# Eight more tokens take their rows of v by gather, and the dense product with v is 168 tokens wide instead of 176

## The chip, the core and the metric

The kernel runs on one core of a Trainium2 chip. The core has a matrix engine (TensorE, PE in the profile, with its weight loads as PEld), a vector engine (VectorE, DVE), an activation engine (ScalarE, ACT), a general engine (GpSimd, POOL) and a queue engine (SyncE, SP). Sixteen DMA engines move data between HBM, the chip's main memory, and SBUF, the core's working memory. TensorE adds up its products in PSUM. The metric is the device time of one execution in microseconds; the number to compare with is the median of several executions.

## The reference, cut to what matters

One decoder layer for 256 tokens of width 1024. A mixer (retention and block attention, merged) comes first. Then each token retrieves experts: 8 heads, 16 experts for each head, out of 16384 experts, each one row of a table u and one row of a table v.

```python
q = (ht @ w_q).reshape(T, PEER_HEADS, 2, half)
s = einsum('thcd,hcnd->thcn', q, sub_keys)
...                                  # top 16 of each half, then top 16 of the sums
experts = take_along_axis(cand_i, pos); gates = softmax(top_s)
u = u_tab[ec]                        # rows of u for the token's 128 experts
a = gelu(einsum('td,thkd->thk', hc, u))
return einsum('thk,thkd->td', gc * a, v_tab[ec])
```

The layer's output is the residual stream plus this last sum.

## The kernel before

**Two ways for one sum.** A token's experts can be fetched row by row (a gather: an indirect DMA that puts 128 rows of 4 KB into the 128 partitions), or the token can go through the dense part, where the whole table passes through the core and TensorE multiplies it with all dense tokens; experts that the token didn't choose get weight zero. The kernel does both. Of its 256 tokens, `NG` = 64 are gathered in u and in v. `NX` = 64 more are gathered in u only, in `NXG` = 4 groups of `NXP` = 16 tokens; one of those groups (`NXV` = 1), the last 16 tokens of the first tile of 128, is gathered in v too. So `NA` = 128 tokens go through the dense product with u, and `ND` = 256 - 64 - 16 = 176 through the dense product with v.

**Gathers.** For the 64 fully gathered tokens one transfer covers one of `NJ` = 64 list positions: 64 tokens and two heads fill the 128 partitions. For a group of 16 tokens the partitions are 8 heads x 16 tokens, and 16 transfers cover the 16 experts of each head. So `NU` = 64 + 64 = 128 transfers fetch rows of u, and `NV` = 64 + 16 = 80 fetch rows of v. Each moves 128 rows of 4 KB, 512 KB. `eg` holds the row numbers, `av` the weights, one column for a transfer. `fetch` (L1049) issues a transfer on GpSimd's queue into one of `RING` = 6 buffers. `gather_step` (L1108) is one step of the sequence: a fetch, and the use of the oldest buffer. For u that is a dot product on VectorE (L1064), for v a weighted sum into an accumulator (L1152): `acc` for the 64 tokens, `accx` for the group of 16, whose first term is written by ScalarE (L1149). Steps are put into the program at a pace, `GATHER` per chunk of the u stage and `GATHER_V` = 0.65 per chunk of the v stage. `later` runs small actions a given number of steps after they were asked for (`after`).

**Small rearrangements.** The lists and gates of the 64 group tokens go through DRAM to change from tokens in partitions to heads x tokens in partitions: `eix` to `eg` (L991, L1089), `gx` to `gg` (L1027, L1097), and the finished weights back into `gates` (L1078, L1083), since three of the four groups use them in the dense product with v. All on GpSimd's queue.

**Dense u stage** (loop L1308). For each of 128 chunks of 128 experts: SP loads 512 KB of u into one of `RAWS` = 6 tiles of `raw_ring`, TensorE transposes it (L730, unless it was turned early) and multiplies it with 128 tokens (L1324), two chunks to a PSUM bank. `HELD` chunks of u are loaded earlier into unused space of W, from chunk row `HELD0`. Meanwhile `dense_gates` (L1208) builds the matrix of gates, 4 tokens a step, 46 rounds of the loop for 176 tokens: one-hot rows on VectorE (L1191, L1194) and ScalarE (L1198), eight small bf16 matmuls (L1249, L1250), and gelu(u h) times gate goes to W, a tile of 128 chunks x `ND` tokens. From chunk row `SCRATCH` on, W serves as scratch space for the choice of the top 16.

**Dense v stage** (loop L1360). For each chunk c: SP loads 512 KB of v (L677) into a raw tile or, from chunk 14 on, into one of two spare places in W that are used up by then, in turns of eight. `cut_v` (L1286) splits the chunk into a high and a low part (ScalarE L151, VectorE L152), two chunks ahead; `cut_w` (L1292) does so with two chunks of W (L1296, L1297). TensorE then does 8 blocks of 128 output columns: one matmul of 2 x `ND` columns (L1356), one of `ND` columns with the low part (L1357), which add up in 8 PSUM banks all through the stage. For the 6 pairs of chunks in `PLAIN` nothing is split: one fp32 matmul of `ND` columns for each block (L1354), straight from the raw tile, which stays taken until then. SP's queue is in order: a load waits for its tile and holds up the next.

**End.** At `FOLD` = 104 the two halves of `acc` are added and written. At chunk 123 any sums left are done and rows of the residual stream are loaded. At chunk 125 eight matmuls with `pick` (L1396) sum `accx` over the 8 heads of each token into PSUM columns beside the others. Then the last two chunks are done block by block, with the turning back, the residual sum and the output.

Of the kernel before, what the change touches and what calls it, by code (L numbers as in the profile page):

```python
# [11 lines left out]
F32 = mybir.dt.float32  # L12
# [10 lines left out]
P = 128  # L23
S = 256
# [9 lines left out]
NXV = 1  # L34
NX = NXP * NXG
NA = S - NG - NX
ND = S - NG - NXP * NXV
RING = 6
GATHER_V = 0.65
GATHER = 1.04  # L40
GATHER_G = 1.14
RAWS = 6
# [3 lines left out]
BUDGET = 1.5  # L46
GSTEP = 2.05
LAG_G = 2
SCRATCH = 88
TOPK = 16  # L50
HELD = [0, 1, 2, 8, 14, 21] + list(range(26, 62, 6)) + [61, 66]
HELD0 = 2
FOLD = 104
TURNED = list(range(10, 38, 2)) + [39, 41, 43, 46, 48, 51, 53, 56, 58, 60, 63, 65, 67, 70]
NPRE = len(TURNED)
# [24 lines left out]
def layer_kernel(ctx, tc, x, mix_norm_g, w_in, ret_w_branch, moba_q_gain, moba_k_gain, moba_w_branch,  # L80
# [788 lines left out]
    av = tk.tile([P, NJ + NX], F32, name="av")  # L869
    eg = tk.tile([P, NJ + NX], I32, name="eg")  # L870
# [196 lines left out]
    def weights_x():  # L1067

        c = slice(NJ, NU)
        gs["x"] = 0  # L1070

        def nonlinear():
            A.activation(av[:, c], av[:, c], AF.Gelu)
            after(2, product)

        def product():
            V.tensor_tensor(av[:, c], av[:, c], gg[:, c], op=OP.mult)
            nc.gpsimd.dma_start(gx[1].rearrange("n h i k -> (h i) n k"), av[:, c].rearrange("p (n k) -> p n k", n=NXG))  # L1078
            after(2, back)

        def back():
            for n in range(NXV, NXG):
                nc.gpsimd.dma_start(x_rows(gates, n), gx[1][n].rearrange("h i k -> i h k"))  # L1083
            gs["xdone"] = True

        after(1, nonlinear)

    def experts_x():
        nc.gpsimd.dma_start(eg[:, NJ:].rearrange("p (n k) -> p n k", n=NXG), eix.rearrange("n h i k -> (h i) n k"))  # L1089

# [17 lines left out]
    def gather_step():  # L1108
# [35 lines left out]
        if weighed and gs["sum"] < gs["v"] and (gs["v"] - gs["sum"] == RING or gs["v"] == NV):  # L1144
            j = v_order[gs["sum"]]
            r = gs["rows"].pop(j)
            if j == NJ:
                gs["accx"] = a = tk.tile([P, D], F32, name="accx", tag="hx")
                A.activation(a, r, AF.Copy, scale=av[:, j:j + 1])  # L1149
            else:  # L1150
                a = gs["acc" if j < NJ else "accx"]
                V.scalar_tensor_tensor(a, r, av[:, j:j + 1], a, op0=OP.mult, op1=OP.add)  # L1152
            gs["sum"] += 1

    V.memset(pick[:, :32 - NXP], 0.0)
    V.tensor_reduce(pick[:, 32 - NXP:], ident.rearrange("p (h i) -> p i h", i=NXP), axis=AX.X, op=OP.add)
    V.tensor_copy(iota4, iota[:, :, None].to_broadcast([P, NK, 4]))
    held = list(HELD)

# [200 lines left out]
    for c in range(NK):  # L1360
# [26 lines left out]
        if c == NK - 5:  # L1387
            while gs["sum"] < NV:
                gather_step()
            r0b, r1 = spare(3), spare(4)  # L1390
            nc.gpsimd.dma_start(r0b[:half], x1d[NG:P - NXP, 0, :])
            nc.gpsimd.dma_start(r1, x1d[:, 1, :])
        if c == NK - 3:
            for b in range(KC):
                s = slice(b % 4 * 32, b % 4 * 32 + 32)
                T.matmul(o[b // 4][s, 2 * ND:2 * ND + P], pick, gs["accx"][:, b * P:(b + 1) * P], start=False, stop=True,  # L1396
                         skip_group_check=True)

    back = {}

# [5 lines left out]
    def turn_back(b):  # L1406
        t = back.pop(b)
        n = slice(b * P, (b + 1) * P)
        T.transpose(o[b][:, :P], t[:, :P], ident)
        T.transpose(o[b][:half, P:2 * P], t[:, P:P + half], ident)  # L1410
        V.tensor_tensor(r1[:, n], r1[:, n], o[b][:, :P], op=OP.add)
        V.tensor_tensor(r0b[:half, n], r0b[:half, n], o[b][:half, P:2 * P], op=OP.add)
        if b < 2:
            V.tensor_tensor(rx[:, b], rx[:, b], o[b][:, 2 * ND:2 * ND + P], op=OP.add)
        if b == 1:
            dst = out_flat[P - NXP:P, :].rearrange("i (q j d) -> j i q d", q=2, j=4)
            for j in range(4):
                nc.gpsimd.dma_start(dst[j], rx[32 * j + 32 - NXP:32 * j + 32])
        if b in (3, 5, 7):
            d = slice({3: 0, 5: 512, 7: 768}[b], P * (b + 1))  # L1420
            nc.sync.dma_start(out_flat[P:, d], r1[:, d])
            q = nc.scalar if b == 7 else nc.sync
            q.dma_start(out_flat[NG:P - NXP, d], r0b[:half, d])

    for b in range(KC):
        for c in (NK - 2, NK - 1):
# [59 lines left out]
```

## Time and profile before

| what | value |
|---|---|
| median of 3 executions | 931.07 us (930.93 to 934.0) |
| the profiled execution, its own time | 932.75 us |
| its span, first to last instruction | 931.0 us |
| mean granted clock of TensorE | 0.998 |
| busy: TensorE / VectorE / ScalarE / GpSimd | 921.5 / 802.5 / 510.9 / 451.0 us |
| moved by DMA | 333.03 MB, 358 GB/s over the span |
| first fetch of v / last fetch of v | 618.1 us / 890.7 us |
| dense u stage, first and last L1324 | about 302 to 641 us |
| dense v stage up to the pick matmuls | about 641 to 919 us |

The profile is of one execution, so a sum of its parts is compared with 931.0 and 932.75, and then with the median. Busy time counts an engine's instructions; a busy TensorE can still be one that waits inside a stream for its next weights. DMA share is the mean busy share of 16 DMA engines. A row of the timeline has the start, the length, the engine, the line and `out<-in`; a row of the waits has the waiting engine and line, what ended the wait, the sum, the count and the longest. "To landing" is the time from the issue of a transfer to the arrival of its last data.

### The profile page before, as it was taken

Reading aid. Unit: us, or ns where it says so; the run is one execution under the profiler, and the core shown is the slowest. Engines: PE = TensorE matmul, PEld = TensorE weight load, DVE = VectorE, ACT = ScalarE, POOL = GpSimd, SP = SyncE. Lnnn points to the kernel's source line nnn. Section 1 sums busy time; section 2 is a strip of 40 time slices with the busy share of each in tenths; the row PEclk is TensorE's granted clock in tenths of the full one; section 3 lists DMA queues with packets and bytes.
Section 4 is the critical chain, followed back from the end, with each engine's and each line's share of the span. In section 5 each row is a group of like instructions: output and inputs, shape, how many; then the busy total and the mean of one; then the engine's idle time right before and its main releaser. Section 6 shows DMA issues by size and latency. Waiting matters only on the chain.

```text
span 931.0 us, 18728 instructions
## 1 busy us (share of the span) xinstructions
PE 921.5 (99%) x6952; PEld 874.4 (94%) x6952; DVE 802.5 (86%) x1539; ACT 510.9 (55%) x938; POOL 451.0 (48%) x420
## 2 busy tenths in 40 slices
PE   9999999999999999999999999999999999999998
PEld 6878888888999999999999999999999999999997
DVE  6658866988879999999899999975999989898996
ACT  5535665534653435434677777775454545454543
POOL 3527324232102447434576687873656554455540
PEclk9999999999999999999999999999999999999999
DMA  9999989999899999999999999999999999999991
GB/s 316 203 295 313 338 299 291 329 345 333 291 366 405 401 379 354 375 380 348 407 401 405 404 384 405 403 388 340 381 399 408 409 404 410 384 409 368 387 391 61
DMA packets 108265, 333.03 MB, mean 358 GB/s; under 512 B 12460, under 2 KB 16469, under 8 KB 108046
## 3 DMA queue, kind: packets, MB, share of 16 engines
q1 hardware_dynamic: 65532, 185.17, 55.3%
q0 software_dynamic: 37824, 129.57, 38.0%
q10 hardware_dynamic: 4818, 17.09, 4.8%
q8 instruction: 55, 0.90, 0.4%
q14 instruction: 36, 0.29, 0.1%
HBM read 313.88 MB, written 19.43 MB: 358 GB/s over the span
## 4 chain that ended last, share of the span: by engine, by line
PE 94%; DMA 5%; ACT 0%; POOL 0%; DVE 0%; issue 0%; SPq 0%; DVEq 0%; ACTq 0%
PE acc L1324 24%; PE side L730 10%; PE acc L1356 9%; PE side L1356 9%; PE acc L234 6%; PE acc L235 6%; PE acc L236 6%; PE acc L1357 4%; PE side L1357 4%; DMA raw_ring<-in_w_in_dram 4%; PE acc L244 2%; PE acc L243 2%; PE acc L245 2%; PE side L1354 2%; PE acc L1354 2%; PE acc L1250 1%
## 5 line engine op out<-in xcount | busy, mean ns | idle before, releaser
L1053 POOL DMA_INDIRECT rows<-in_peer_u_dram,eg x86 | 109.0, 1267 | 72.9 <-DVE rows L1064 27.0
L1053 POOL DMA_INDIRECT rows<-in_peer_v_dram,eg x54 | 97.1, 1799 | 76.6 <-DVE vacc L1152 58.7
L730 PE MATMUL side<-ident,raw_ring 128*128 128x128 f32 x688 | 92.3, 277 | 1.3 <-DMA raw_ring<-in_peer_u_dram 1.3
L730 PEld LDWEIGHTS side<-ident,raw_ring 128*128 128x128 f32 x688 | 83.4, 192 | 1.5 <-issue 1.5
L1296 ACT ACTIVATE cw<-W 128x352 fp32r<-128x352 f32 x58 | 28.9, 499 | 74.7 <-PE acc L1357 74.7
L1198 ACT ACTIVATE oh_buf<-oh_more,tS 128x128 bf16<-128x128 f16 x176 | 58.4, 416 | 0.7 <-DVE oh_more L1191 0.5
L1064 DVE SCALAR_TENSOR_TENSOR rows<-rows,h 128x1024 f32<-128x1024 f32 x44 | 55.0, 1260 | 1.4 <-DMA rows<-in_peer_u_dram,eg 1.4
L1324 PE MATMUL acc<-hTd,raw_ring 128*128 128x128 f32 x448 | 54.6, 275 | 0.0
L1152 DVE SCALAR_TENSOR_TENSOR vacc<-rows,av,vacc 128x1024 f32<-128x1024 f32 x42 | 53.7, 1279 | 0.1
L1324 PEld LDWEIGHTS acc<-hTd,raw_ring 128*128 128x128 f32 x448 | 52.3, 192 | 0.0
L1297 DVE TENSOR_TENSOR cw<-W,cw 128x352 fp32r<-128x352 f32 x58 | 30.2, 521 | 20.0 <-ACT cw L1296 19.5
L740 POOL DMA_DIRECT2D h<-in_peer_u_dram x40 | 21.9, 552 | 44.3 <-DVE hTf L744 32.5
L1282 POOL TENSOR_TENSOR W<-W,gl 128x256 f32<-128x256 f32 (+21 forms) x32 | 26.7, 833 | 29.4 <-ACT gl L1281 24.6
L740 POOL DMA_DIRECT2D eraw<-in_peer_u_dram x40 | 22.0, 555 | 27.3 <-DVE eT L744 16.5
L1191 DVE TENSOR_TENSOR oh_more<-iota,tI 128x1024 f16<-128x1024 f16 x44 | 34.3, 780 | 0.0
L1194 DVE TENSOR_TENSOR oh_buf<-oh_more,tM 128x1024 f16<-128x1024 f16 x44 | 33.0, 751 | 0.0
L1250 PE MATMUL acc<-oh_buf 128*128 128x128 bf16 x176 | 24.4, 219 | 0.0
L1249 PE MATMUL acc<-oh_buf 128*128 128x128 bf16 x176 | 24.4, 219 | 0.0
L1265 ACT ACTIVATE W<-acc 128x512 f32<-128x512 f32 (+22 forms) x44 | 17.3, 392 | 12.8 <-PE acc L1250 11.7
L1284 ACT ACTIVATE W<-acc 128x256 f32<-128x256 f32 (+21 forms) x53 | 18.5, 349 | 5.5 <-PE acc L1324 5.4
L1249 PEld LDWEIGHTS <-oh_buf 128*128 128x128 f16 x176 | 19.8, 114 | 0.0
L1250 PEld LDWEIGHTS <-oh_buf 128*128 128x128 f16 x176 | 19.7, 114 | 0.0
(2599 smaller groups left out, 3394.2 us busy)
## 6 DMA issues: line engine op xcount, KB each, us to landing
raw_ring<-in_peer_v_dram SPq DMA_DIRECT2D x100, 512.0 KB, 10.1
raw_ring<-in_peer_u_dram SPq DMA_DIRECT2D x86, 512.0 KB, 8.3
raw_ring<-in_w_in_dram SPq DMA_DIRECT2D x52, 512.0 KB, 7.9
raw_ring<-turned SPq DMA_DIRECT2D x28, 512.0 KB, 10.8
W<-in_peer_v_dram SPq DMA_DIRECT2D x28, 512.0 KB
raw_ring<-in_peer_w_q_dram SPq DMA_DIRECT2D x16, 512.0 KB, 9.3
W<-in_peer_u_dram SPq DMA_DIRECT2D x14, 512.0 KB, 10.7
eraw<-in_peer_u_dram POOLq DMA_DIRECT2D x40, 128.0 KB, 7.5
```

The costliest lines, as they stand in the source:

```text
L234: T.matmul(o[t], xh[:, s], wh, start=(k == 0), stop=False)
L235: T.matmul(o[t], xh[:, s], wl, start=False, stop=False)
L236: T.matmul(o[t], xl[:, s], wh, start=False, stop=(k == kc - 1))
L730: T.transpose(p[:, k * P:(k + 1) * P], r.rearrange("p (i k) -> p k i", k=KC)[:, 4 * q + k], ident)
L1053: G.indirect_dma_start(out=r, out_offset=None, in_=tab, in_offset=bass.IndirectOffsetOnAxis(ap=eg[:, j:j + 1], axis=0))
L1064: V.scalar_tensor_tensor(r, r, 1.0, h, op0=OP.mult, op1=OP.mult, accum_out=av[:, j:j + 1])
L1152: V.scalar_tensor_tensor(a, r, av[:, j:j + 1], a, op0=OP.mult, op1=OP.add)
L1198: A.activation(o1[:, j], hot[:, 0, :, j], AF.Copy, scale=tS[:, t, k + j:k + j + 1])
L1250: T.matmul(p[:, j * P:(j + 1) * P], lo, o1, start=False, stop=True)
L1324: T.matmul(pa[:, n:n + NA], uT[:, k * P:(k + 1) * P], hT[:, k], start=(c % 2 == 0 and k == 0), stop=(k == KC - 1), skip_group_check=True)
L1356: T.matmul(o[b][:, :2 * ND], vh[:, n], w, start=(c == 0), stop=False, skip_group_check=True)
L1357: T.matmul(o[b][:, :ND], vl[:, n], w[:, :ND], start=False, stop=(c == NK - 1), skip_group_check=True)
```

## The change

Eight more tokens, `NY` = `NXP` // 2, the second half of another group of 16, have their rows of v gathered. The partitions of their transfers are 2 halves of the list x 8 heads x 8 tokens, so that eight transfers cover the 16 experts of each head. `NV` goes from 80 to 88 and `ND` from 176 to 168. Their lists (`eiy`) and weights (`gy`) take six small transfers through DRAM (`halves`, `listed`, `last`). They get an accumulator of their own, `accy`, started by ScalarE, and a second `pick` that sums it over halves and heads, so 16 pick matmuls instead of 8. The gate matrix has 42 steps instead of 44. The pace `GATHER_V` goes from 0.65 to 0.71. The plain pairs are 7, 17, ... instead of 6, 16, ...; held rows start at chunk row 0 of W and the scratch space at 86; the spare places in W are counted in elements, since a chunk row of W is now 168 long. The output of the 24 tokens is written in four transfers as that of the 16 was, and the dense rows of the first tile are 40 instead of 48.

```diff
-ND = S - NG - NXP * NXV
+NY = NXP // 2
+ND = S - NG - NXP * NXV - NY
-GATHER_V = 0.65
+GATHER_V = 0.71
-SCRATCH = 88
+SCRATCH = 86
-HELD0 = 2
+HELD0 = 0
-NV = NJ + NXP * NXV
-PLAIN = [6 + 10 * i for i in range(6)]
+NV = NJ + NXP * NXV + NY
+PLAIN = [7 + 10 * i for i in range(6)]
...
-        return W[:, 6 * n:6 * n + 6, :].rearrange("p c t -> p (c t)")[:, :D]
+        return W.rearrange("p c t -> p (c t)")[:, D * n:D * n + D]
...
-    v_order = range(NV)
-    pick = tk.tile([P, 32], F32, name="pick")
+    v_order = [*range(NJ + NXP * NXV), *range(NU, NU + NY)]
+    pick = [tk.tile([P, 32], F32, name=f"pick{i}") for i in range(2)]
+    accy = tk.tile([P, D], F32, name="accy")
+
+    def halves(dst, src):
+
+        src = src[NXG - 1][:, NXP - NY:, :].rearrange("h i (b k) -> b h i k", b=2)
+        for b in range(2):
+            nc.gpsimd.dma_start(dst[b], src[b])
...
+            halves(gy, gx[1])
             gs["xdone"] = True
+            after(3, last)
+
+        def last():
+            nc.gpsimd.dma_start(av[:, NU:], gy.rearrange("b h i k -> (b h i) k"))
...
+        halves(eiy, eix)
...
             ready[gs["u"]:gs["u"]] = range(NJ, NU)
+            nc.gpsimd.dma_start(eg[:, NU:], eiy.rearrange("b h i k -> (b h i) k"))
...
-            if j == NJ:
-                gs["accx"] = a = tk.tile([P, D], F32, name="accx", tag="hx")
+            if j in (NJ, NU):
+                if j == NJ:
+                    gs["accx"] = tk.tile([P, D], F32, name="accx", tag="hx")
+                a = gs["accx"] if j == NJ else accy
                 A.activation(a, r, AF.Copy, scale=av[:, j:j + 1])
             else:
-                a = gs["acc" if j < NJ else "accx"]
+                a = accy if j > NU else gs["acc" if j < NJ else "accx"]
...
-                T.matmul(o[b // 4][s, 2 * ND:2 * ND + P], pick, gs["accx"][:, b * P:(b + 1) * P], start=False, stop=True,
-                         skip_group_check=True)
+                for a, n in zip((gs["accx"], accy), pick):
+                    T.matmul(o[b // 4][s, 2 * ND:2 * ND + P], n, a[:, b * P:(b + 1) * P], start=False, stop=True,
+                             skip_group_check=True)
```

More of the change, by code (lines that the diff above doesn't have):

```diff
@@ L170, in layer_kernel @@
     eix = dr.tile([NXG, H, NXP, TOPK], I32, name="eix")
+    eiy = dr.tile([2, H, NY, TOPK // 2], I32, name="eiy")
+    gy = dr.tile([2, H, NY, TOPK // 2], F32, name="gy")
     gx = [dr.tile([NXG, H, NXP, TOPK], F32, name=f"gx{i}") for i in range(2)]
@@ L868, in layer_kernel @@
     ei = tk.tile([P, NT, NP], I32, name="ei")
-    av = tk.tile([P, NJ + NX], F32, name="av")
-    eg = tk.tile([P, NJ + NX], I32, name="eg")
+    av = tk.tile([P, NU + NY], F32, name="av")
+    eg = tk.tile([P, NU + NY], I32, name="eg")
     gg = tk.tile([P, NJ + NX], F32, name="gg")
@@ L1083, in back @@
                 nc.gpsimd.dma_start(x_rows(gates, n), gx[1][n].rearrange("h i k -> i h k"))
+            halves(gy, gx[1])
             gs["xdone"] = True
+            after(3, last)
+        def last():
+            nc.gpsimd.dma_start(av[:, NU:], gy.rearrange("b h i k -> (b h i) k"))
         after(1, nonlinear)
     def experts_x():
-        nc.gpsimd.dma_start(eg[:, NJ:].rearrange("p (n k) -> p n k", n=NXG), eix.rearrange("n h i k -> (h i) n k"))
+        halves(eiy, eix)
+        nc.gpsimd.dma_start(eg[:, NJ:NU].rearrange("p (n k) -> p n k", n=NXG), eix.rearrange("n h i k -> (h i) n k"))
         def listed():
             ready[gs["u"]:gs["u"]] = range(NJ, NU)
+            nc.gpsimd.dma_start(eg[:, NU:], eiy.rearrange("b h i k -> (b h i) k"))
         after(3, listed)
@@ L1146, in gather_step @@
             r = gs["rows"].pop(j)
-            if j == NJ:
-                gs["accx"] = a = tk.tile([P, D], F32, name="accx", tag="hx")
+            if j in (NJ, NU):
+                if j == NJ:
+                    gs["accx"] = tk.tile([P, D], F32, name="accx", tag="hx")
+                a = gs["accx"] if j == NJ else accy
                 A.activation(a, r, AF.Copy, scale=av[:, j:j + 1])
             else:
-                a = gs["acc" if j < NJ else "accx"]
+                a = accy if j > NU else gs["acc" if j < NJ else "accx"]
                 V.scalar_tensor_tensor(a, r, av[:, j:j + 1], a, op0=OP.mult, op1=OP.add)
             gs["sum"] += 1
-    V.memset(pick[:, :32 - NXP], 0.0)
-    V.tensor_reduce(pick[:, 32 - NXP:], ident.rearrange("p (h i) -> p i h", i=NXP), axis=AX.X, op=OP.add)
+    for a, n, i in zip(pick, (32 - NXP, 32 - NXP - NY), (NXP, NY)):
+        V.memset(a, 0.0)
+        V.tensor_reduce(a[:, n:n + i], ident.rearrange("p (h i) -> p i h", i=i), axis=AX.X, op=OP.add)
     V.tensor_copy(iota4, iota[:, :, None].to_broadcast([P, NK, 4]))
@@ L1390, in layer_kernel @@
             r0b, r1 = spare(3), spare(4)
-            nc.gpsimd.dma_start(r0b[:half], x1d[NG:P - NXP, 0, :])
+            nc.gpsimd.dma_start(r0b[:half], x1d[NG:NG + half, 0, :])
             nc.gpsimd.dma_start(r1, x1d[:, 1, :])
@@ L1415, in turn_back @@
         if b == 1:
-            dst = out_flat[P - NXP:P, :].rearrange("i (q j d) -> j i q d", q=2, j=4)
+            dst = out_flat[P - NXP - NY:P, :].rearrange("i (q j d) -> j i q d", q=2, j=4)
             for j in range(4):
-                nc.gpsimd.dma_start(dst[j], rx[32 * j + 32 - NXP:32 * j + 32])
+                nc.gpsimd.dma_start(dst[j], rx[32 * j + 32 - NXP - NY:32 * j + 32])
         if b in (3, 5, 7):
@@ L1422, in turn_back @@
             q = nc.scalar if b == 7 else nc.sync
-            q.dma_start(out_flat[NG:P - NXP, d], r0b[:half, d])
+            q.dma_start(out_flat[NG:NG + half, d], r0b[:half, d])
     for b in range(KC):
```

## The prediction

> **What bounds the kernel now.** I read the page first: busy shares, the 40 slices, the shares of the chain of waits.
>
> ```profile
> span 931.0 us, 18728 instructions
> ...
> PE 921.5 (99%) x6952; PEld 874.4 (94%) x6952; DVE 802.5 (86%) x1539; ACT 510.9 (55%) x938; POOL 451.0 (48%) x420
> ...
> GB/s 316 203 295 313 338 299 291 329 345 333 291 366 405 401 379 354 375 380 348 407 401 405 404 384 405 403 388 340 381 399 408 409 404 410 384 409 368 387 391 61
> ...
> PE 94%; DMA 5%; ACT 0%; POOL 0%; DVE 0%; issue 0%; SPq 0%; DVEq 0%; ACTq 0%
> ```
>
> TensorE is hardly ever idle, so the chain runs along it. But from the middle of the span on, the DMA rate stops again and again near 405 to 410 GB/s. The change takes work from TensorE and gives work to DMA, so the question is what room DMA has in the stage that changes most, the product with v. Busy time by stretch, in the order PE, PEld, DVE, ACT, POOL, then clock, DMA share, GB/s; below it the DMA traffic of 640 to 910 us:
>
> ```profile
> 640.00:660.00 20.00, 20.00 (x152) 20.00 (x151) 18.18 (x19) 13.28 (x17) 10.82 (x7) 1.00 0.97 357
> 660.00:680.00 20.00, 20.00 (x147) 20.00 (x145) 18.10 (x18) 8.29 (x11) 12.15 (x7) 1.00 1.00 384
> 680.00:800.00 120.00, 120.00 (x877) 120.00 (x876) 110.96 (x110) 61.13 (x74) 65.17 (x36) 1.00 1.03 408
> 800.00:880.00 80.00, 80.00 (x583) 80.00 (x582) 72.61 (x73) 43.85 (x54) 44.24 (x28) 1.00 1.00 384
> 880.00:910.00 30.00, 30.00 (x219) 30.00 (x218) 29.19 (x29) 13.97 (x17) 10.53 (x8) 1.00 1.00 382
> ```
>
> ```profile
> DMA packets 29162, 105.99 MB, mean 393 GB/s; under 512 B 3313, under 2 KB 3313, under 8 KB 29137
> ```
>
> TensorE is busy all the time, so today it sets the pace. DMA held 408 GB/s for 120 us, which I take as its ceiling here. At 408 the 105.99 MB need 259.8 us of the 270, so about 10.2 us of DMA time is unused: 2.5 in the first 20 us, 1.2 in the next, 4.7 in 800 to 880, 1.9 in the last 30.
>
> **TensorE, the part removed.** For a chunk of 128 experts that isn't plain, each of 8 blocks is a pair: 352 columns (L1356), then 176 (L1357). First and last L1356 of 23 pairs in a row; then first and last of 27 intervals of 512 columns, and of 43 intervals of 256 columns, in earlier stages:
>
> ```profile
> 679.70 0.35 PE L1356 MATMUL side<-cw,rhi__7544 128*128 128x352 f32 x1
> ...
> 685.97 0.35 PE L1356 MATMUL side<-cw,rhi__7615 128*128 128x352 f32 x1
> ```
>
> ```profile
> 199.83 0.39 PE L236 MATMUL acc<-rhi__1780,rl 128*128 128x512 f32 x1
> ...
> 205.95 0.39 PE L236 MATMUL acc<-rhi__1848,rl 128*128 128x512 f32 x1
> ```
>
> ```profile
> 264.78 0.28 PE L243 MATMUL acc<-hh,rhi__2411 128*128 128x256 f32 x1
> ...
> 269.94 0.28 PE L244 MATMUL acc<-hl,rhi__2454 128*128 128x256 f32 x1
> ```
>
> A pair takes 6.27/23 = 272.6 ns. Matmuls of 512 columns follow each other at 226.7 ns, of 256 at 120.0, so a column costs 0.417 ns and a matmul 13.3 ns beside its columns. By that line 352 columns are 160 ns and 176 are 86.7, together 246.7. The pair has 26 ns more: as if the second took 112 ns. Passes of 128 fp32 columns (L730, in the fence on plain chunks below) also stand at 0.89/8 = 111 ns, whence my estimate that a matmul can't be shorter than about 112 ns here, since its next weights have to be loaded meanwhile. Then only the wide half shrinks: 16 columns, 6.7 ns a pair. If both halves shrink, it is 24 columns, 10.0 ns. With 116 such chunks of 8 pairs, that is 6.2 or 9.3 us; I take 6.2, because of those 26 ns.
>
> The Trainium skill ("TensorE: Matmul & The Clock Gate", LDWEIGHTS) gives a load of 128 weight columns as 128/1.2 = 107 ns, near the 112 ns; the same page (Back-to-back issue gap) has N/2.4 + 2.5 ns for a matmul alone, by which both halves would shrink and the stage would give 9.3 us. The pair's 272.6 ns against 225 by that formula speaks for the load.
>
> The 12 plain chunks (L1354) make two passes for each block. In the chain of waits in order of time (start, length, what), eight transposes of the u stage, a plain chunk's two rows, and the start of the next plain pair:
>
> ```profile
> 321.24 0.89 PE side L730 x8
> ...
> 667.72 1.22 PE side L1354 x8
> 668.95 1.19 PE acc L1354 x8
> ...
> 711.74 1.22 PE side L1354 x8
> ```
>
> 176 columns take 1.20/8 = 150 ns a pass, 128 take 111, so 0.8 ns a column and 6.4 ns a pass for 8 columns; 12 x 8 x 2 passes give 1.2 us. The period of 20 chunks, 711.74 - 667.72 = 44.0 us, falls to 44.0 - 144 x 0.0067 - 32 x 0.0064 = 42.9 us (42.4 if both halves shrink). Over the stage TensorE saves 6.2 + 1.2 = 7.4 us (at most 10.5).
>
> Building the gate matrix has two steps fewer, 16 bf16 matmuls. Eight follow each other in 563.13 - 562.68 = 0.45 us, so 0.9 us is saved near the end of the u stage, just before its one wait:
>
> ```profile
> 562.68 0.22 PE L1249 MATMUL acc<-oh_buf 128*128 128x128 bf16 x1
> ...
> 563.13 1.11 PE L730 MATMUL side<-ident,raw_ring 128*128 128x128 f32 x8
> ```
>
> ```profile
> PE side L730 <- DMA raw_ring<-in_peer_u_dram: 1.3, 1, 1.3
> ```
>
> TensorE may only wait longer there, for a transfer. Bounds 0 and 0.9 us; I take 0.5, the middle. The eight added pick matmuls stand at the end with nothing over them. The eight there now take 0.64 us:
>
> ```profile
> 918.69 0.64 PE L1396 MATMUL side<-accx,pick 128*32 128x128 f32 x16
> ```
>
> So at most +0.6 us, which I take (the lower bound is 0, if they overlap).
>
> **DMA, the part added.** Eight gathers of 128 rows of 4 KB are 4.19 MB: 10.3 us at 408 GB/s. 105.99 + 4.19 = 110.18 MB need 270.1 us, the whole of today's 270, and TensorE would like to be 7.4 us sooner. In steady state 20 chunks ask for 20 + 14.2 transfers, 17.9 MB in 42.9 us: 418 GB/s, over the ceiling. So TensorE's saving can't all be had. What remains is the delay that the buffers can take up: the loads may land later, against the end of the stage.
>
> ```profile
> 897.62 2.44 SPq L677 DMA_DIRECT2D raw_ring<-in_peer_v_dram  x2
> ...
> 914.89 1.04 ACT L151 ACTIVATE rhi__10040<-raw_ring 128x1024 fp32r<-128x1024 f32 x1
> ```
>
> ```profile
> DMA to landing us min/median/max: 6.6/9.1/12.1
> ```
>
> ```profile
> DMA to landing us min/median/max: 7.1/13.4/14.8
> ```
>
> The last load is issued at about 900.1 (897.62 + 2.44) and lands, by the median of 880 to 910 us (upper line), at 909.2; it is first read at 914.9, so 5.7 us could be given away. At 680 to 720 us (lower line) landings already took 13.4 us in the median and TensorE didn't wait, so delays of this size can be borne. ScalarE felt them:
>
> ```profile
> ACT rhi__7485 L151 <- DMA raw_ring<-in_peer_v_dram: 4.4, 1, 4.4
> ACT rhi__7940 L151 <- DMA raw_ring<-in_peer_v_dram: 4.2, 1, 4.2
> ```
>
> A later load is such a wait at ScalarE's cut (L151). Behind it stand the cut of W (L1296) and, on VectorE, the low part (L152) and the weighted sums; SP's next load into that tile and GpSimd's next gather wait for these. So the end is late only when the two cut chunks in hand run out. The unused 2.5 us of 640 to 660 stays, since no gather can start before sums free its buffers. The other 7.7 us can be filled, as gathers and loads both queue. The stage: 270.1 + 2.5 - 5.7 = 266.9, a gain of 3.1 us.
>
> The Trainium skill ("DMA: Bandwidth & Descriptors", Measured) has 425 GB/s for large loads; at that rate 418 GB/s would fit and TensorE's whole 7.4 us would show. The trace's 408 over 120 us, with shares of 1.03, speaks against it.
>
> **What costs nothing.** VectorE does eight more weighted sums less one (the first is ScalarE's), and 42 instead of 44 gate steps:
>
> ```profile
> L1152 DVE SCALAR_TENSOR_TENSOR vacc<-rows,av,vacc 128x1024 f32<-128x1024 f32 x42 | 53.7, 1279 | 0.1
> ```
>
> In 680 to 800 us VectorE has 110.96 of 120 busy; 54.5 chunks bring 0.06 x 54.5 = 3.3 more sums, 4.2 us, 115.2 in about 117 to 119: 97 to 98%. It fits, barely; without that cover it costs up to 7 x 1.28 = 9 us. Six small transfers on GpSimd's queue are like these:
>
> ```profile
> L991 POOL DMA_DIRECT2D eix<-ei x4: 548/553/609, 348.8 to 350.4; - x4
> ```
>
> Six times 0.55 us on a queue whose gathers run up to six ahead of their use; the two that read a list wait for landings that L1089 and L1083 wait for already, and behind them stand the next gather and the products of L1282. I take 0; uncovered, 3.3 us. The pace ends where it did: 88 sums at 0.71 a chunk are done at chunk 123, as 80 were at 0.65. The other edits (where spare tiles lie in W, which pairs are plain, the start of the held rows) move bytes between buffers; no instruction is added.
>
> **Sum.** Stage -3.1, gates -0.5, pick +0.6: -3.0 us, the span 931.0 becomes 928.0. The profiled execution took 932.75 us, 1.75 around its span and 1.68 over the median; the median 931.07 becomes 928.1.
>
> **Rivals.**
> *TensorE's pace holds.* The buffers (six raw tiles, two in W, six of rows) absorb the shortage until the gathers end. For it: no wait of TensorE in the stage even at 13.4 us of landing, and 408 may be what was asked for and not the ceiling; against: 418 over 408. Gain 7.4 + 0.9 - 0.6 = 7.7 us, 923.4; with both halves shrinking 10.8, 920.3.
> *Swallowed.* Of the 10.2 us unused, 5.5 stay: 270.1 + 5.5 - 5.7 = 269.9, so 931.0.
> *Slower: SP's queue starves DMA.* A plain chunk keeps its raw tile until TensorE is through with it, and SP, in order, waits:
>
> ```profile
> SPq L677 <- PE acc L1354: 51.9, 12, 7.3
> ```
>
> If these waits make the gaps of 800 to 880 us, and all six plain pairs, which now lie in raw tiles, make such gaps again, all 10.2 us stay: 270.1 + 10.2 - 5.7 = 274.6, with the rest +4.7, 935.8. It decides from about 6 us of kept gaps on. Against it: at 711 and 755 us a plain pair left no gap, the loads still out covered it.
>
> **How the numbers follow.** Forecast, a part of the gain (926.4 to 930): 0.47. TensorE's pace: 0.24, of it 0.04 for both halves. Swallowed (930 to 934): 0.18. Slower: 0.11. The bound of what can be told from no change is 0.5%, 4.7 us: 926.4 and 935.7. Faster is the second case and a little of the first, 0.27; slower the last, and not all of it, 0.10; same 0.63. The range 922.5 to 935.0 leaves out the both-halves case and most of the last.
>
> **What would show it.** After the change: starts of L1356 266 ns apart (262.6 would be both halves); the stage's DMA at 405 or more in nearly every stretch after 660; landings of L677 at 13 us and over late in the stage; ScalarE waiting for raw tiles past 720, and some idle TensorE at L1356. TensorE without idle time there and DMA over 415 GB/s would prove the second case; gaps at plain pairs with DMA under 395 the last.

## The result and the profile after

The kernel after takes 936.16 us (median of 15 runs, 930.08 to 941.88), the kernel before 930.55 us on the same chip (15 runs, 927.53 to 934.0). The ratio is 1.0061, with a 95% interval of 1.0043 to 1.0078: 5.6 us slower, where 928.1 and a gain of 3.0 were forecast. The profiled execution after took 941.88 us, the longest of its runs. One execution of a kernel below, "narrow only", took 2052 us and is not counted in its ratio (without it that kernel's median is 925.62). From here on "cut" means the split of a chunk by ScalarE and VectorE, and line numbers of the kernel after are used: L1376 and L1377 are the pair, L1374 the plain passes, L152 and L153 the cuts, L1171 the weighted sum, L1404 the addition at the fold, L1417 the pick. Rows of a changed kernel have its own numbers, a few lines off (L1380 and L1321 with eight loads less are L1376 and L1317 here); a kernel made from the one before has its numbers.

The page of the kernel after, busy shares, the GB/s of the 40 slices and the shares of the chain of waits:

```profile
span 940.0 us, 18745 instructions
...
PE 920.3 (98%) x6952; PEld 870.4 (93%) x6952; DVE 807.0 (86%) x1544; ACT 509.3 (54%) x929; POOL 476.2 (51%) x434
...
GB/s 307 212 282 285 336 299 302 328 351 334 282 363 402 390 394 342 375 398 338 408 407 406 401 362 407 404 389 349 405 408 408 407 408 409 408 408 409 386 375 62
...
PE 70%; DMA 18%; DVE 6%; issue 4%; ACT 1%; SPq 0%; DVEq 0%; POOL 0%; ACTq 0%; POOLq 0%
```

TensorE's share of the chain fell from 94% to 70%, and DMA's rose from 5% to 18%. In the stage of v nearly every slice now stands at 405 to 409 GB/s. The stretches of the prediction from 660 us on, with the last 40 us divided more finely (columns: PE, PEld, DVE, ACT, POOL, clock, DMA share, GB/s):

```profile
660.00:680.00 20.00, 20.00 (x150) 19.91 (x148) 19.18 (x20) 7.98 (x11) 14.38 (x8) 1.00 1.03 411
680.00:800.00 120.00, 118.56 (x881) 117.45 (x879) 114.03 (x114) 63.04 (x76) 75.64 (x38) 1.00 1.03 408
800.00:880.00 80.00, 78.58 (x581) 77.54 (x579) 74.41 (x75) 41.39 (x50) 50.68 (x31) 1.00 1.03 408
880.00:890.00 10.00, 6.15 (x43) 5.95 (x42) 7.25 (x8) 4.98 (x6) 4.81 (x3) 0.89 1.03 356
890.00:900.00 10.00, 10.00 (x61) 10.00 (x61) 7.36 (x7) 2.21 (x2) 9.21 (x4) 0.77 1.02 399
```

DMA moved 408 GB/s from 680 to 880 us without a break; before, the stretch from 800 on had 384. TensorE is no longer always busy: 1.4 us idle in each of the two long rows, and 3.85 us in 880 to 890, after which its granted clock falls to 0.89 and 0.77.

The start of every plain pair cuts the stage into periods of 20 chunks. The first pass of the first two and the last two in the timeline of the kernel after, and the first and the last row of the pick:

```profile
673.84 1.33 PE L1374 MATMUL side<-W,raw_ring 128*128 128x168 f32 x8
717.67 1.34 PE L1374 MATMUL side<-W,raw_ring 128*128 128x168 f32 x8
...
849.87 1.34 PE L1374 MATMUL side<-W,raw_ring 128*128 128x168 f32 x8
900.05 1.34 PE L1374 MATMUL side<-W,raw_ring 128*128 128x168 f32 x8
...
925.95 0.45 PE L1417 MATMUL side<-accx,pick 128*32 128x128 f32 x8
...
926.62 0.44 PE L1417 MATMUL side<-accy,pick 128*32 128x128 f32 x8
```

Four periods take 43.8 to 44.2 us, as long as before (44.0) and not 42.9. The fifth, with the fold in it, takes 50.2. From the first matmul of the stage (643.9) to the pick it is 282.1 us, against 277.4 before.

Set side by side, the two profiled executions differ by 941.88 - 932.75 = 9.1 us: the stage of v +4.7, from the pick to the end of the span 14.1 against 12.3, +1.8, the stage of u 338.5 against 339.0, -0.5, and the start of the stage of u +3.0 (305.4 against 302.4); 0.1 lies around the span. The start of the stage of u shows no effect of the change: in the profiles of the experiments that start lies between 298.0 and 301.4, with the eight tokens and without. (In both executions here TensorE's granted clock was down near 62 us: 0.66 from 60 to 65 us before, 0.68 and 0.63 from 60 to 70 us after.) Without these two 6.0 are left, about the 5.6 of the medians.

**How the fold stalls.** At chunk 104 GpSimd sends half of `vacc` (the accumulator of the 64 tokens) into W, and at chunk 107 VectorE adds it. VectorE in the timeline of the kernel after, then ScalarE, then TensorE (the brackets hold the idle time before and what ended it):

```profile
881.92 1.28 DVE L1171 SCALAR_TENSOR_TENSOR accx<-rows,av,accx 128x1024 f32<-128x1024 f32 x1
885.95 1.22 DVE L1404 TENSOR_TENSOR W<-W,vacc 64x1024 f32<-64x1024 f32 x1 [2.75 <-DMA W<-vacc]
887.09 1.21 DVE L153 TENSOR_TENSOR rlo__9675<-raw_ring,rhi__9674 128x1024 fp32r<-128x1024 f32 x1
888.23 0.49 DVE L1317 TENSOR_TENSOR cw<-W,cw 128x336 fp32r<-128x336 f32 x1
```

```profile
880.66 1.06 ACT L152 ACTIVATE rhi__9674<-raw_ring 128x1024 fp32r<-128x1024 f32 x1 [1.31 <-DMA raw_ring<-in_peer_v_dram]
```

```profile
884.50 0.35 PE L1376 MATMUL acc<-cw,rhi__9649 128*128 128x336 f32 x1
884.68 0.24 PE L1377 MATMUL acc<-cw,rlo__9650 128*128 128x168 f32 x1
888.77 0.65 PE L1376 MATMUL side<-cw,rhi__9674 128*128 128x336 f32 x1 [3.85 <-DVE cw L1317]
...
889.36 0.56 PE L1376 MATMUL side<-cw,rhi__9674 128*128 128x336 f32 x1
```

ScalarE had its half of the next chunk ready at 881.7. VectorE stood 2.75 us at L1404, then added, and only then made the low half (887.09) and cut W (888.23). TensorE, which finished the chunk before, had nothing to do for 3.85 us. After that its pairs stand about 0.5 us apart (888.77, 889.36, and on to 894.29) instead of 0.27, for some 6 us. The transfer itself was no slower than before. Tile `vacc`, its transfer and the addition, before and after:

```profile
L1378 POOL DMA_DIRECT2D W<-vacc x1: 580/580/580, 870.3 to 870.3; - x1
L1384 DVE TENSOR_TENSOR W<-W,vacc x1: 1218/1218/1218, 879.8 to 879.8; 64x1024 f32<-64x1024 f32 x1
...
  DMA W<-vacc: 1.4, 1
```

```profile
L1398 POOL DMA_DIRECT2D W<-vacc x1: 563/563/563, 876.6 to 876.6; - x1
L1404 DVE TENSOR_TENSOR W<-W,vacc x1: 1218/1218/1218, 886.0 to 886.0; 64x1024 f32<-64x1024 f32 x1
...
  DMA W<-vacc: 2.8, 1
```

From issue to addition it is 9.5 us before and 9.4 after, and the low half and the cut of W behind it are done 12.3 us after the issue before (at 882.6), 12.1 after (888.7). VectorE waited at the fold before, too, for 1.4 us. It cost nothing, because TensorE wanted that chunk only 13.0 us after the issue:

```profile
883.30 0.35 PE L1356 MATMUL side<-cw,rhi__9673 128*128 128x352 f32 x1
```

So the fold of before had 0.7 us to spare. After the change TensorE was through with the chunk ahead of it at 884.9, 8.3 us after the issue, 3.8 too soon. The stock of finished work had shrunk: in the chunks from 865 us to the fold, VectorE finished a low part 2.9 to 4.2 us ahead of TensorE's first use of it in the kernel before, and 0.3 to 1.5 us ahead after the change. ScalarE's part of the very next chunk had itself just waited 1.31 us for its load. What takes the stock away, DMA or something else, is for the experiments.

### The profile page after: what moved, and what is told of

Its sections match the earlier page's. It is cut to its first block, busy times and chain, and to the rows that moved or that the text cites. A ratio compares the mean times of both kernels' runs of the same rounds, so it can differ in the third digit from the quotient of the medians.

```text
span 940.0 us, 18745 instructions
## 1 busy us (share of the span) xinstructions
PE 920.3 (98%) x6952; PEld 870.4 (93%) x6952; DVE 807.0 (86%) x1544; ACT 509.3 (54%) x929; POOL 476.2 (51%) x434
## 4 chain that ended last, share of the span: by engine, by line
PE 70%; DMA 18%; DVE 6%; issue 4%; ACT 1%; SPq 0%; DVEq 0%; POOL 0%; ACTq 0%; POOLq 0%
PE acc L1344 23%; DMA raw_ring<-in_peer_v_dram 11%; PE side L733 9%; PE acc L237 6%; PE acc L238 6%; PE acc L239 6%; DMA W<-in_peer_v_dram 3%; DMA raw_ring<-in_w_in_dram 3%; PE side L1376 2%; PE acc L1376 2%; DVE vacc L1171 2%; PE acc L246 2%; PE acc L247 2%; PE acc L248 2%; PE acc L1270 1%
## 5 line engine op out<-in xcount | busy, mean ns | idle before, releaser
L1063 POOL DMA_INDIRECT rows<-in_peer_v_dram,eg x58 | 111.7, 1926 | 68.7 <-DVE vacc L1171 49.0
L1063 POOL DMA_INDIRECT rows<-in_peer_u_dram,eg x86 | 106.2, 1234 | 76.0 <-DVE rows L1074 31.3
L1218 ACT ACTIVATE oh_buf<-oh_more,tS 128x128 bf16<-128x128 f16 x168 | 55.8, 418 | 1.0 <-DVE oh_more L1211 1.0
L1171 DVE SCALAR_TENSOR_TENSOR vacc<-rows,av,vacc 128x1024 f32<-128x1024 f32 x42 | 53.6, 1277 | 0.1
L743 POOL DMA_DIRECT2D h<-in_peer_u_dram x40 | 21.8, 552 | 46.8 <-DVE hTf L747 33.6
L1317 DVE TENSOR_TENSOR cw<-W,cw 128x336 fp32r<-128x336 f32 x58 | 29.0, 499 | 11.7 <-ACT cw L1316 11.7
L1316 ACT ACTIVATE cw<-W 128x336 fp32r<-128x336 f32 x58 | 27.5, 474 | 16.4 <-PE acc L1377 14.9
L743 POOL DMA_DIRECT2D eraw<-in_peer_u_dram x40 | 22.0, 554 | 28.1 <-DVE eT L747 16.5
L1214 DVE TENSOR_TENSOR oh_buf<-oh_more,tM 128x1024 f16<-128x1024 f16 x42 | 30.0, 714 | 0.0
L1269 PE MATMUL acc<-oh_buf 128*128 128x128 bf16 x168 | 23.3, 219 | 0.0
L1270 PE MATMUL acc<-oh_buf 128*128 128x128 bf16 x168 | 23.3, 219 | 0.0
L1287 DVE TENSOR_TENSOR W<-acc,W 128x256 f32<-128x256 f32 (+21 forms) x32 | 16.1, 502 | 4.9 <-ACT W L1285 4.2
L996 POOL DMA_DIRECT2D eg<-ei x4 | 2.3, 564 | 34.5 <-ACT W L634 30.7
```

Source lines behind the costliest of these rows:

```text
L743: queue.dma_start(dst[32 * g:32 * g + 32].rearrange("a (b d) -> a b d", b=4), src[g])
L1063: G.indirect_dma_start(out=r, out_offset=None, in_=tab, in_offset=bass.IndirectOffsetOnAxis(ap=eg[:, j:j + 1], axis=0))
L1218: A.activation(o1[:, j], hot[:, 0, :, j], AF.Copy, scale=tS[:, t, k + j:k + j + 1])
```

## The experiments

The table has, from each kernel's profile, the time from the first matmul of the v stage to the first plain pair, the five periods of 20 chunks, the rest to the pick, and their sum, in us. Each profile is of one execution. "Ratio" is the time against executions of the kernel before on the same chip, with its 95% interval; it differs from the ratio of the two medians, by 0.2% at most.

| kernel | periods of the v stage | sum | median | ratio |
|---|---|---|---|---|
| before | 26.2, 44.0, 44.0, 44.0, 44.0, 44.0, 31.0 | 277.4 | 930.55 | |
| after | 29.9, 43.8, 44.2, 44.0, 44.0, 50.2, 25.9 | 282.1 | 936.16 | 1.0061 (1.0043 to 1.0078) |
| narrow only | 29.8, 42.8, 42.8, 42.8, 43.2, 44.5, 25.9 | 271.8 | 925.66 | 0.9937 (0.9913 to 0.996) |
| gathers only | 26.2, 44.0, 44.0, 44.0, 44.9, 46.2, 31.0 | 280.4 | 934.48 | 1.005 (1.0032 to 1.0067) |
| eight loads less | 30.0, 42.9, 43.0, 42.8, 42.8, 48.9, 25.9 | 276.2 | 930.42 | 1.000 (0.9983 to 1.0017) |
| half sums | 29.8, 42.8, 43.5, 43.8, 44.9, 50.7, 25.9 | 281.3 | 935.5 | 1.0057 (1.0034 to 1.0079) |
| fold later | 30.0, 43.7, 44.2, 43.4, 44.9, 43.8, 30.1 | 279.9 | 935.93 | 1.0082 (1.0047 to 1.0118) |
| before, fold later | 27.1, 44.0, 44.0, 44.0, 44.0, 44.0, 31.0 | 278.2 | 930.42 | 1.0003 (0.9984 to 1.0022) |
| eight loads less, fold later | 29.9, 43.1, 42.8, 42.8, 42.8, 42.8, 25.9 | 270.1 | 924.83 | 0.9952 (0.9933 to 0.997) |
| plain pairs at 6 | 25.7, 43.8, 44.0, 43.7, 44.7, 49.7, 30.1 | 281.6 | 937.37 | 1.0093 (1.0061 to 1.0125) |
| four tokens | 30.2, 43.4, 43.4, 43.4, 43.4, 48.9, 26.3 | 278.9 | 939.92 | 1.0103 (1.0088 to 1.0119) |
| four tokens, fold later | 30.9, 43.4, 43.4, 43.4, 43.4, 43.4, 27.7 | 275.6 | 935.58 | 1.0054 (1.0041 to 1.0067) |
| before, pace 0.71 | 26.3, 44.0, 44.0, 44.0, 44.0, 46.8, 31.0 | 280.2 | 934.29 | 1.004 (1.0026 to 1.0055) |
| before, pace 0.71, fold later | 26.2, 44.0, 44.8, 44.0, 44.0, 44.2, 31.0 | 278.2 | 930.97 | 1.0003 (0.9988 to 1.0019) |
| four tokens, lists later | 32.9, 43.4, 43.4, 43.4, 43.4, 43.4, 28.1 | 278.1 | 930.06 | 0.9996 (0.9984 to 1.0009) |

### One half of the change at a time

The kernel after without the eight tokens' gathers and sums, at the old pace; their part of the output is left out (`accy` is only set to zero):

```diff
-GATHER_V = 0.71
+GATHER_V = 0.65
...
-NV = NJ + NXP * NXV + NY
+NV = NJ + NXP * NXV
...
```

> The changed kernel without its eight added gathers and their sums (accy is only set to zero, so the retrieval of eight tokens is left out), paced at 0.65: the removed part alone. DMA theory (the v stage is held at 408 GB/s): 20 + 13 transfers in 42.9 us are 403 GB/s, just under the ceiling, so TensorE sets the pace and the time is 923 to 926 us against 930.5 of before. VectorE theory (it is 97% full in the changed kernel): 13 sums in 20 chunks leave it at 94%, so also 923 to 927. If the narrower product itself is no cheaper, 929 to 931.

The kernel before with eight more gathers (of rows that it fetches anyway) and their sums, which go nowhere:

```diff
-GATHER_V = 0.65
+GATHER_V = 0.71
...
-NV = NJ + NXP * NXV
+NV = NJ + NXP * NXV + 8
...
+            elif gs["sum"] > NV - 8:
+                V.scalar_tensor_tensor(r, r, av[:, j:j + 1], r, op0=OP.mult, op1=OP.add)
```

> The kernel before with eight more gathers of v rows and eight more scalings of them (into their own buffers; the result doesn't use them), paced at 0.71: the added part alone, the product still 176 wide. DMA theory: 110.2 MB need 270 us at 408 GB/s and the stage is 277 us to the pick matmuls, so there is room on average, 930 to 934 us. VectorE theory: 41.9 us in a period of 44.0 are 95%, so 930 to 932. If the added gathers cost their full 10.3 us, 940.

The narrow product alone gains 4.9 us, and its stage of v 5.6; its first periods are 42.8 us, what the prediction's 42.9 had worked out for TensorE. The gathers alone lose 3.9 us, a little more than either theory allowed, 3.0 of it in the fourth and fifth period, though TensorE's work is unchanged. So the gain is there. But the two halves do not add up: 277.4 - 271.8 = 5.6 gained and 280.4 - 277.4 = 3.0 lost would leave a gain of 2.6 in the stage of v, and measured is a loss of 4.7. A faster TensorE leaves DMA less time for the same bytes.

### What is short: bytes, VectorE, or SP's queue

Eight loads of v are left out, as many bytes as the eight gathers bring; those chunks are multiplied with their neighbour's rows:

```diff
+SKIPPED = [24, 40, 48, 64, 72, 80, 88, 104]
...
+            if c in SKIPPED:
+                v_raw[c] = v_raw[c - 1]
```

> The changed kernel with eight loads of v chunks left out, spread over the stage (those chunks use their neighbour's rows, so the product is another one): the bytes of before with all of the changed kernel's work on the engines. DMA theory: the waits for landings and TensorE's idle time at L1376 go, 923 to 927 us. VectorE theory: as the changed kernel, 934 to 938.

The weighted sums take only half of the columns, so that half of the output of the gathered tokens is missing:

```diff
-                V.scalar_tensor_tensor(a, r, av[:, j:j + 1], a, op0=OP.mult, op1=OP.add)
+                V.scalar_tensor_tensor(a[:, :D // 2], r[:, :D // 2], av[:, j:j + 1], a[:, :D // 2], op0=OP.mult, op1=OP.add)
```

> The changed kernel with the weighted sums of v rows on 512 of the 1024 columns (the other half of these tokens' retrieval is left out): VectorE has about 86 x 0.6 = 50 us less to do, the bytes are the same. DMA theory: as the changed kernel, 933 to 938 us. VectorE theory: 923 to 927.

The plain pairs stand where they stood before:

```diff
-PLAIN = [7 + 10 * i for i in range(6)]
+PLAIN = [6 + 10 * i for i in range(6)]
```

> The changed kernel with the plain pairs at 6, 16, ... as before. If the place of the plain pairs matters (a plain chunk holds its raw tile while SP waits), 2 us or more of difference, in either direction; if the bytes and the stall are all, 934 to 937 us as the changed kernel.

Bytes it is, in the ordinary periods: with eight loads less these fall to 42.8 to 43.0 us, while with half the sums they go up to 44.9 all the same, and the time is that of the kernel after. (A load left out also frees SP's queue and a raw tile for a while; no run takes away the bytes alone.) The place of the plain pairs changes nothing that these runs can tell. ScalarE's idle time before the cut of v, 640 to 920 us, by what ended it: the kernel before, after, and after with eight loads less:

```profile
  DMA raw_ring<-in_peer_v_dram: 18.0, 9
  DMA W<-in_peer_v_dram: 2.0, 2
```

```profile
  DMA raw_ring<-in_peer_v_dram: 60.6, 49
  DMA W<-in_peer_v_dram: 24.0, 13
```

```profile
  DMA raw_ring<-in_peer_v_dram: 21.4, 15
  DMA W<-in_peer_v_dram: 15.3, 9
```

The cut waits for a load 62 times after the change, instead of 11 times, and 24 times with the bytes given back. But that run still has a period of 48.9 us, the one with the fold, and so its 930.42 us lie above the 923 to 927 that the DMA theory expected.

### The fold

VectorE's addition comes six chunks later and the transfer of its result five, so that `vacc` has landed when VectorE gets there; tried on the kernel after, on the kernel before, and with eight loads less:

```diff
-        if c == FOLD + 3:
+        if c == FOLD + 9:
...
-        if c == FOLD + 8:
+        if c == FOLD + 13:
```

> The changed kernel with the add of the two halves of vacc (VectorE's wait for the transfer W<-vacc) six chunks later, at chunk 113, and the write of it at chunk 117; the same work and bytes. Theory of the stall: VectorE, in order, waits 2.8 us for that transfer, TensorE runs dry for 3.9 us and then has half its clock for 6.8 us, so about 6 us go, 928 to 931 us. Pure DMA theory: the bytes set the pace and the lost time only reappears as other waits, 934 to 937.

> The kernel before with the same move of the add from chunk 107 to 113. Both theories: there VectorE waited 1.4 us and TensorE not at all, so no difference, 929 to 932 us; if it is clearly faster, some of before's executions had that stall too.

> The changed kernel with eight loads of v chunks left out (those chunks use their neighbour's rows) and with the add moved to chunk 113. Theory of two causes, bytes and the stall at the add: with both gone TensorE sets the pace, 923 to 926 us. If the stall was only a sign of the bytes: as with the loads alone, 930.

TensorE's waits, 600 to 930 us, in the kernel after (whole span), with the fold later, with eight loads less, and with both:

```profile
PE side L1376 <- DVE cw L1317: 6.6, 8, 3.9
```

```profile
PE side L1376 <- DVE cw L1317: 5.6, 12, 1.0
```

```profile
PE side L1380 <- DVE cw L1321: 2.8, 1, 2.8
```

```profile
PE side L737 <- DMA raw_ring<-in_peer_u_dram: 1.6, 1, 1.6
```

With eight loads less, the fold alone is left, and moving it gains 930.42 - 924.83 = 5.6 us: 2.8 of waiting and the rest at the lower clock. With both gone no wait is left in the stage of v (the one in the last fence is of the stage of u), and it takes 270.1 us; TensorE's pace by the prediction was 277.4 - 7.4 = 270.0. With all the bytes, moving the fold gains nothing that these runs can tell (935.93 us, as the pure DMA theory had it): eight waits of 6.6 us in all, one of them 3.9, become twelve of 5.6 in all, none over 1.0, and the last segment is 30.1 us instead of 25.9. DMA is as late as it was, and the delay shows somewhere else. Before the change the fold cost nothing.

The shortage of bytes is not all that brings the stall. With eight loads less VectorE has its low parts ready 2.4 to 3.4 us ahead, nearly as before, and still TensorE runs dry for 2.8 us. The transfer and the addition in that run:

```profile
L1402 POOL DMA_DIRECT2D W<-vacc x1: 563/563/563, 866.3 to 866.3; - x1
L1408 DVE TENSOR_TENSOR W<-W,vacc x1: 1218/1218/1218, 876.5 to 876.5; 64x1024 f32<-64x1024 f32 x1
```

TensorE is out of work at 876.5, when the addition only begins: 10.2 us after the issue, where the kernel before gave it 13.0. So the transfer is issued later against TensorE's work than it was. The faster pace of the gathers is a candidate, since it changed here too, and the next runs test it.

### The pace alone, and half the tokens

The kernel before, with its 80 gathers at the pace that 88 need, first with nothing else, then with the fold later:

```diff
-GATHER_V = 0.65
+GATHER_V = 0.71
```

> The kernel before with the pace of the weighted sums alone raised from 0.65 to 0.71 a chunk: no transfer more, the 80 gathers are spread over less of the stage (done by chunk 113 instead of 123). Theory that DMA's ceiling decides: 20 chunks ask for 17.9 MB, 44.0 us at 408 GB/s, just what TensorE needs with 176 columns; the last 10 chunks have loads alone: 930 to 932, ratio 1.000 to 1.002. Rival, that the pace itself (six buffers that come round faster, waits at the fold) made the loss: 933 to 936, ratio 1.003 or more.

> The kernel before with the pace 0.71 and, beside it, the fold's addition nine steps later; nothing is left out. With the pace alone it took 934.3 us and its stage of v 2.9 us more than before's 277.4, all in the period that has the fold (46.8 us against 44.0). Theory, that this is the stall at the fold and the half clock after it, since DMA at 408 GB/s still carries 44.0 us a period: stage 277 to 278, time 930 to 932, ratio 0.999 to 1.001. Rival, that the delay of the loads is only met elsewhere, as with the eight tokens, where moving the fold gained nothing: 933 to 935, ratio 1.003 to 1.005, with waits in the last segment.

The pace alone, with no byte more, loses 3.7 us, nearly as much as the pace and the gathers together (3.9). My expectation of 930 to 932 fell, and the rival (waits at the fold) held. TensorE's waits in the stage, then three stretches, of the kernel before at pace 0.71:

```profile
PE side L1356 <- DVE cw L1297: 2.6, 1, 2.6
```

```profile
680.00:800.00 120.00, 120.00 (x875) 120.00 (x875) 115.04 (x114) 63.15 (x75) 82.42 (x40) 1.00 1.03 409
800.00:880.00 80.00, 80.00 (x584) 80.00 (x583) 73.74 (x74) 42.62 (x51) 49.01 (x28) 1.00 1.03 406
880.00:890.00 10.00, 7.45 (x54) 7.24 (x53) 8.61 (x8) 3.29 (x4) 1.62 (x3) 1.00 1.02 336
```

DMA is full here too (409 and 406), and just keeps up: the periods stay at 44.0. But the low parts are ready only 1.1 to 2.2 us ahead, TensorE is out of work 9.1 us after the issue of the fold's transfer (872.5) instead of 13.0, and the fold costs 2.6 us. With the fold later it is 930.97, no different from before. So for the pace alone, at the old width, the stall at the fold was the whole loss. How much of the lost lead is the full DMA and how much the place of the transfer among the gathers on GpSimd's queue isn't separated.

Last, four tokens instead of eight, whose DMA should just keep up with TensorE. Their lists come in quarters instead of halves, the accumulator lies in a spare place of W, and the scratch space and the held rows start one chunk row further on:

```diff
-NY = NXP // 2
+NY = NXP // 4
...
-GATHER_V = 0.71
+GATHER_V = 0.68
...
```

> Nothing is left out: 4 more tokens instead of 8 have their rows of v gathered, in four transfers of a quarter of a list for each head, the dense product is 172 wide, the pace 0.68. TensorE: the wide matmul loses 8 columns, 3.3 ns a pair, 116 x 8 of them 3.1 us, and the plain passes 192 x 3.2 ns = 0.6 us; a period of 20 chunks would be 43.45 us. DMA: 20 + 13.6 transfers of 524 KB in a period, 17.6 MB, 43.2 us at 408 GB/s. Theory that DMA's ceiling of 408 GB/s took the gain (and the wait at the fold the rest): here the ceiling lies just under TensorE's pace, so most of the 3.7 us shows, less 1.5 us behind the last output and some of the fold's stall: 928 to 930, ratio 0.997 to 1.000. Rival, each added transfer costs time by itself wherever the ceiling lies: half of the change's loss, 933, ratio 1.003.

> The same with four more tokens, and the addition at the fold nine steps later, its output transfer thirteen steps after the fold's start. Theory: without the stall at the fold the rest is TensorE's pace, periods of 43.4 to 43.6 us also in the one that has the fold: 926 to 928, ratio 0.995 to 0.998, and 1 to 4 us below the run with the fold where it was. Rival (transfers cost by themselves): 931 to 933, and moving the fold gains nothing, as it gained nothing with eight tokens.

Both were wrong in the sum, theories and rivals alike, and right in the stage of v: its periods are 43.4 us, TensorE's pace, but for the one with the fold (48.9), and with the fold later it takes 275.6. But the stage of u took 344.2 us instead of 339.0. VectorE's longest wait there, 520 to 580 us, with the fold later:

```profile
DVE rows__6036 L1074 <- DMA rows__6036<-in_peer_u_dram,eg: 6.4, 1, 6.4
```

GpSimd in the timeline of the same run, around the gather that came late:

```profile
546.87 1.71 POOL L1093 DMA_DIRECT2D gates<-gx  x3
548.52 2.23 POOL L935 DMA_DIRECT2D gy<-gx  x4
555.29 1.02 POOL L1063 DMA_INDIRECT rows__6036<-in_peer_u_dram,eg  x1 [4.53 <-DVE oh_more L1211]
```

Behind seven small transfers in a row the gather stands 4.53 us, and VectorE behind it 6.4. With eight tokens, where `gy` takes two transfers and not four, the gather behind them stood 0.30 us:

```profile
551.57 1.19 POOL L935 DMA_DIRECT2D gy<-gx  x2
553.07 1.74 POOL L1063 DMA_INDIRECT rows__6033<-in_peer_u_dram,eg  x1 [0.30 <-DMA rows<-in_peer_u_dram,eg]
```

What GpSimd waits for isn't settled: the operation named in the bracket is VectorE's one-hot rows, which have no data for the gather. In the next run the small transfers come later, the weights' when only two gathers of u are left, and the lists' after them (the diff shows the weights):

```diff
-            halves(gy, gx[1])
             gs["xdone"] = True
-            after(3, last)
+            after(26, partial(halves, gy, gx[1]))
+            after(30, last)
...
```

> Four more tokens, fold later, and the small transfers of their lists and weights issued 26 steps and more after the gates' own, when no gather of u is behind them on GpSimd's queue; nothing is left out. In the run before this the stage of v was 275.7 us, 1.7 less than before, but the stage of u 344.1 against 339.0, with VectorE waiting 6.4 us for one gather of u. Theory, that the small transfers delayed that gather: u stage 338.5 to 339.5, v stage 275 to 276.5, tail 1 us more than before: 929 to 931, ratio 0.998 to 1.000. Rival, that 43 steps of the gate matrix instead of 44 or 42 put the order of the gates out: u stage still 343 to 345, time 934 to 936.

The long wait is gone, the u stage takes 336.8 us, and the time is 930.06 us, 5.5 less. The v stage took 278.1 us (275 to 276.5 expected), 2.4 more than in the run before it, 2.0 of that in the first segment, and the u stage took less than expected; from the first matmul with u to the pick it is 614.9 us, against 616.3 before. The tail is 1.2 us longer, and the gain is gone: no version here that computes the whole output beats the kernel before.

## Why the prediction was wrong

**TensorE's part: right.** The first of 17 starts of L1376 in a row after the change, and the last:

```profile
678.66 0.35 PE L1376 MATMUL side<-cw,rhi__7517 128*128 128x336 f32 x1
...
682.91 0.35 PE L1376 MATMUL side<-cw,rhi__7548 128*128 128x336 f32 x1
```

4.25/16 = 265.6 ns a pair, 7.0 less than 272.6, where 6.7 were forecast and 10.0 if both halves shrank. So only the wide half shrinks. The Trainium skill's time for loading 128 columns, 128/1.2 = 107 ns ("TensorE: Matmul & The Clock Gate", LDWEIGHTS), agrees with it, though no run shows that the load is the reason. The period of 42.8 and the 270.1 us of the undisturbed stage (7.2 less than before) bear out the sum of 7.4 us.

**The ceiling: right.** 408 GB/s held for 200 us, and giving bytes back was what brought the pace back. The Trainium skill has 425 GB/s for large loads ("DMA: Bandwidth & Descriptors", Measured); no long stretch of these runs reached it. 17.9 MB at 408 are 44.0 us, so the gain in a period had to be zero as long as gathers run. "TensorE's pace holds" is refuted.

**The step that failed** is "what remains is the delay that the buffers can take up ... so 5.7 us could be given away". It counted the whole delay against the end of the stage, and took the slack of the last load for the slack of all. ScalarE near the end of the run with eight tokens and the fold later, where the stall is away and that step should have held (pick at 917.1):

```profile
907.36 1.06 ACT L152 ACTIVATE rhi__9956<-raw_ring 128x1024 fp32r<-128x1024 f32 x1 [1.10 <-DMA raw_ring<-in_peer_v_dram]
...
912.62 1.05 ACT L152 ACTIVATE rhi__10044<-raw_ring 128x1024 fp32r<-128x1024 f32 x1
```

The last load that ScalarE waits for is the fifth from the end, cut at 907.36. The four after it came in time, so the slack of the last one didn't help those before it. That stage took 279.9 us, 9.8 over TensorE's pace, where 4.3 were forecast. The difference is nearly the 5.7: without it the prediction's own sum gives 270.1 + 2.5 = 272.6, 2.6 over today's 270, a stage of 277.4 + 2.6 = 280.0. That is one profiled execution, the fastest of six, so the agreement to a tenth is luck; the size is not.

**What was not seen** is that the delay need not wait for the end. "So the end is late only when the two cut chunks in hand run out" was true, and they ran out at the fold. I had costed VectorE by its busy share (it "fits, barely"); the run with half sums shows that its work indeed wasn't the limit. But it works in order, and its wait of 1.4 us for `vacc` stood in the trace of before, with 0.7 us to spare behind it. At the new width and pace, with the bytes given back, this wait is worth 5.6 us; without them, the delay that isn't paid there is paid later. The two don't add up, and how the 4.7 us of the kernel after divide between them can't be told from these runs.

**The signs came, the time didn't.** Starts 266 ns apart, DMA at 405 or more, ScalarE waiting past 720 us and some idle time at L1376 were named as what would show the forecast, and all of them appeared. They show that DMA is full; they don't show what that costs.

**Slower, by SP's queue:** its 935.8 was near by luck, its mechanism wrong. It needed gaps of DMA at the plain pairs; there are none, 408 in 680 to 800 and 800 to 880. It isn't idle DMA that costs the time, but what waits behind a full one.

**The small terms.** The 0.5 us for the gate steps can't be told from the spread: the stage of u takes 338.5 us after and 339.0 before, but over all profiles 338.1 to 339.2 with 42 steps and 337.4 to 339.0 with 44. The added pick matmuls cost 0.5 (from 925.95 to 926.62 + 0.44 = 927.06, 1.1 us against 0.64). From the pick to the end of the span the kernels with a second `pick` take 13.1 to 14.1 us, those without 12.3 to 12.6; beyond the pick's 0.5 the cause wasn't found. That the six small transfers cost nothing fits the eight tokens' stage of u, and was not safe: with ten of them, for four tokens, it took 5 us more, and moving them brought that back.

## What to carry to other kernels

When one stage asks DMA for all that it can carry, work it out by the period, bytes against the time that the other engine would like, and don't pay the shortage from the slack of the last load. Then look through the trace of before for short waits of in-order engines that cost nothing now: they live on a stock of finished work, and a change can use that up. How much is to spare can be read there (0.7 us here), from the wait to the next engine's use of the result. A transfer that an in-order engine will wait for belongs far ahead of its use (nine chunks here, not three), above all in a stage where landings take 9 us and more.

## What the runs showed of the hardware

A short idle time of TensorE was paid twice here. The start of the first matmul after the fold with eight loads less, and the stretch after it:

```profile
879.29 0.65 PE L1380 MATMUL side<-cw,rhi__9666 128*128 128x336 f32 x1 [2.80 <-DVE cw L1321]
```

```profile
880.00:885.00 5.00, 5.00 (x22) 5.00 (x22) 5.00 (x6) 2.21 (x2) 4.30 (x1) 0.50 1.03 398
885.00:890.00 5.00, 5.00 (x36) 5.00 (x36) 2.78 (x3) 0.00 (x0) 4.69 (x3) 0.91 0.84 268
```

2.80 us of idle time halved the granted clock for more than 5 us (0.50, and 0.91 over the next 5 us). In the kernel before at pace 0.71, 2.6 us of idle time did not: its row of 880 to 890 us, above, has 1.00. In all profiles with a longer idle time at the fold, 2.8 to 4.1 us, the clock was at half behind it: by the traces' clock records for 6.8 us in the kernel after, with eight loads less and with half sums, and for 3.4 us with the plain pairs at 6 and with four tokens. One gap's length doesn't decide alone: near 61 us in the kernel before, idle times of 1.08 and 0.76 us with one matmul between them were followed by a clock of 0.50 (62 to 64 us). The Trainium skill gives an idle window of about 3.4 us, at no fixed time, after which the clock is halved ("TensorE: Matmul & The Clock Gate", What's actually happening); here a gap shorter than that was enough. The runs of the kernel after spread over 11.8 us, those of the kernel before over 6.5. Over the 15 runs after, the time and the mean granted clock are correlated at -0.83, so that the long runs are those with the lower clock. How much of that comes from the fold isn't shown: the longest, which is the profiled one, had the lower clock near 62 us as well as behind the fold.
